# Attention's heads at later places in a hand-written order, and four small reorderings of copies, in a decoder block on one core

## The chip, the cores and the metric

The kernel runs on one core of a Trainium2 chip. The metric is the device time of one execution in microseconds (us); less is better. A core has a matrix engine (PE, with its weight loads as PEld), a vector engine (DVE), a scalar engine (ACT), GpSimd (POOL) and a queue that issues transfers (SP). Each engine works through its own list of instructions in order and waits where an instruction needs a result of another engine or of a transfer (DMA). Matmuls write to PSUM, which DVE and ACT read.

## What is computed

One layer for 512 tokens of width 2048, in float32: a token mixer, then a mixture of experts. The reference, cut to the mixer:

```python
h = _rms(x, attn_norm_g)
proj = h @ w_in        # q, six k/v of 4 groups, gates, 1024 pooled columns, 2 x 2048 merge columns
q = rope(rms(q)); k_slc = rope(rms(k_slc)); k_swa = rope(rms(k_swa))
kc, vc = compress(k_cmp), compress(v_cmp)          # 31 blocks
o = g0 * attn(q, kc, vc) + g1 * attn(q, k_slc, v_slc) + g2 * attn(q, k_swa, v_swa)
attn_branch = einsum("bshd,hde->bshe", o, w_head_out)      # 16 heads, 4 per k/v group
pooled = trailing means over 2, 4, 8, 16 positions, minus the token
pool_branch = einsum("bsgc,gce->bsge", pooled, w_pool) * pool_scale
merge = sigmoid(merge_logits)
y = merge[0] * attn_branch + merge[1] * pool_branch
x = x + y @ w_out
x = x + moe(rms(x))                                # 16 experts, two per token
```

With 512 tokens every block is selected and the window holds all keys, so both attentions are causal ones.

## The kernel before

Every float32 product is made of three matmuls: an operand is split into a rounded high part (ACT copies it, line 196) and the rest (DVE or POOL subtract, line 197), and `mm3` (lines 133 to 136) adds hi x hi, hi x lo and lo x hi. Tiles named `hi_...` and `lo_...` are those parts.

The order of the work is written by hand; no scheduler moves anything. `run(main, side)` walks a list of **main pieces**: one piece is one block of weights with its matmuls, in two parts of 12 matmuls of 512 columns (in some pieces one part of 24). After each part it takes one **step**: one entry from the list `deferred` (small DVE work of a piece that has just ended) and one entry from the list `side`. In the attention `side` holds the **slots** of `attention_slots`. A main piece may need a mark, and then `run` takes steps with no matmuls of a main piece between them until the mark is set.

The main pieces in this stretch are `qkv` (queries, keys and values of a group), `u` (pooled columns), `wp` (the pool's map, results `pm`), and `z0` to `z15` (merge columns of 128 output rows each). `z12` waits for the mark `att3`, `z8` for `att2`, `z4` for `att1`, `z0` for `att0`; head h of group g sets it in its last slot. When a `z` ends, DVE multiplies two tiles (line 947), ACT takes a tanh (948), DVE combines (949) and POOL or DVE adds (950).

A head counts its slots from its start w. `at_qk` writes the scores of query tile qt at w + 0, 2, 4, 6 into the one tile `S`; DVE adds the mask, takes the maximum and scales it (lines 772 to 776), ACT takes two exps (778), and only then may the next scores be written. `at_scale` makes the factors and scales the exps (`p`) one or two slots later (783 to 787). `at_T` transposes `p` at w + 9 to w + 14 into the one tile `tr`, which ACT (`pth`, 139) and DVE (`ptl`, 140) read; `at_pv` adds into the one tile `o` at w + 11 to w + 16, the last one copying `o` into `oh` and `ol`; `at_out` at w + 18 maps them (`a`), copies the result and stores it, and sets the mark after the fourth head. A group's start adds, from six slots ahead, transposes of queries (`at_q`, result `qT`) and keys (`at_k`) and the compressed branch (`at_c0` to `at_c4`). The table `PLAN` gives each group's start (`w0`) and the distances of its heads (`hp`).

`pool_out` reads each `pm` out of PSUM, on ACT (922) and DVE (920) in turn, into two buffers of the tag `ao`, which are shared with `a` and free again when the transfer out of them, issued by ACT (924, 831), has landed.

Of the kernel before, what the change touches and what calls it, by code (L numbers as in the profile page):

```python
# [22 lines left out]
NT = 4  # L23
# [3 lines left out]
NKV = 4  # L27
# [14 lines left out]
    'side': 'mnab.Bcd.gD.........h.k.iw',  # L42
    'main': 'ghqqKqKqKVqKVqVVq',
    'kvt': [1, 0, 1, 0],
    'w0': [7, 46, 85, 126],
    'hp': [[8, 8, 9], [8, 8, 9], [8, 8, 9], [8, 8, 8]],
    'q': -6,
    'pv': [11, 13, 14, 15, 16, 16],
    'T': [9, 10, 11, 12, 13, 14],
# [27 lines left out]
def hybrid_block_kernel(  # L77
# [10 lines left out]
    V, A, T, G = nc.vector, nc.scalar, nc.tensor, nc.gpsimd  # L88
# [7 lines left out]
    mix = mix_pool.__enter__()  # L96
# [7 lines left out]
    pools = {}  # L104
# [13 lines left out]
    def f(ap):  # L118
        return ap.bitcast(F32)
# [79 lines left out]
    deferred = []  # L199
# [82 lines left out]
    invb = mix.tile([128, S], F32, name="invb")  # L282
    rtmp = mix.tile([128, 24], F32, name="rtmp")
    gates = mix.tile([128, NT, 48], F32, name="gates")
    vcr = mix.tile([128, NKV, 64], F32, name="vcr")
    kcT = mix.tile([128, 128], F32, name="kcT")
    xt = [early.tile([128, D], F32, tag=f"x{t}", name=f"xt{t}") for t in range(NT)]
    sqx = early.tile([128, NT, 4], F32, name="sqx")
# [29 lines left out]
    hmask = mix.tile([128, 4], F32, name="hmask")  # L318
    icnt = mix.tile([128, 16], F32, name="icnt")
    sc = mix.tile([128, 5, 2, 8], F32, name="sincos")  # L320
    gain = mix.tile([128, 6, 64], F32, name="gain")
    posi = early.tile([128, 5], I32, name="posi")
    gainc = early.tile([128, 64], F32, name="gainc")
    w2k = early.tile([128, 2, 64], F32, name="w2k")
# [14 lines left out]

    def late_loads():  # L340
        q = nc.sync
        for i in range(4):
            q.dma_start(gain[:, i], q_norm_g.to_broadcast([128, 64]))
        q.dma_start(gain[:, 4], k_norm_slc_g.to_broadcast([128, 64]))
        q.dma_start(gain[:, 5], k_norm_swa_g.to_broadcast([128, 64]))
# [244 lines left out]
    def qkv(g):  # L590
        def loads(raw, k0):
            r = [(raw[:, :, 0:256], wcols(k0, 2, C_Q + 256 * g, 256))]
            for i, c in enumerate((C_KS, C_KW, C_VS, C_VW)):
                r.append((raw[:, :, 256 + 64 * i:320 + 64 * i], wcols(k0, 2, c + 64 * g, 64)))
            return r

        def done(ps):
            if g == 0:
                open_att()
            att = pools["att"]  # L600
            qn = QN[g] = att.tile([128, NT, 6, 64], F32, tag="qn", name=f"qn{g}")
            vt = VT[g] = att.tile([128, NT, 2, 128], F32R, tag="vt", name=f"vt{g}", bufs=2)
            ss = att.tile([128, 2, NT, 6], F32, tag="ss", name=f"ss{g}")
            for t in range(NT):
                pv = ps[t][:, 384:512].rearrange("p (b d) -> p b d", b=2)
                A.mul(qn[:, t].rearrange("p h d -> p (h d)"), ps[t][:, 0:384], inv[:, t:t + 1])
                A.mul(vt[:, t, :, 0:64], pv, inv[:, t:t + 1])
                V.scalar_tensor_tensor(vt[:, t, :, 64:128], pv, inv[:, t:t + 1], f(vt[:, t, :, 0:64]),
                                       op0=OP.mult, op1=OP.subtract)
            q2 = qn.rearrange("p t h d -> p (t h) d")  # L610
            q3 = qn.rearrange("p t h d -> p t (h d)")
            rs = ss[:, 1].rearrange("p t h -> p (t h)")
            s2 = ss[:, 0].rearrange("p t h -> p (t h)")

            def squares(u):
                sq = att.tile([128, 12, 64], F32, tag="th", name=f"sq{g}_{u}", bufs=3)
                us = slice(12 * u, 12 * u + 12)
                V.tensor_mul(sq, q2[:, us], q2[:, us])
                V.tensor_reduce(s2[:, us], sq, axis=AX.X, op=OP.add)

            def inverse():
                V.tensor_scalar(s2, s2, 1.0 / HD, EPS, op0=OP.mult, op1=OP.add)
                rsqrt(rs, s2, rtmp)

            def norm():
                V.tensor_tensor(q2, q2, rs[:, :, None].to_broadcast([128, NT * 6, 64]), op=OP.mult)

            def gains():
                V.tensor_tensor(q3, q3, gain.rearrange("p h d -> p (h d)")[:, None, :].to_broadcast([128, NT, 384]),
                                op=OP.mult)  # L630

            def rope():
                rt = att.tile([128, 4, NT, 6, 8], F32, tag="th", name=f"rt{g}", bufs=3)
                x1, x2 = qn[:, :, :, 0:8], qn[:, :, :, 8:16]
                co = sc[:, 0:4, 0, None, :].to_broadcast([128, NT, 6, 8])
                si = sc[:, 0:4, 1, None, :].to_broadcast([128, NT, 6, 8])
                V.tensor_mul(rt[:, 0], x1, co)
# [100 lines left out]
    def at_c4(g):  # L738
        att = pools["att"]
        smt = pools["sm"].rearrange("p t h n -> p t (h n)")  # L740
        ptc = tr_tile(f"pc{g}")
        for t in range(NT):
            T.transpose(ptc[:, t * 128:(t + 1) * 128], smt[:, t], ident)
        pch = att.tile([128, S], F32R, tag="pch", name=f"pch{g}")
        pcl = att.tile([128, S], F32R, tag="pcl", name=f"pcl{g}")
        evac_split(pch, pcl, ptc)
        PC[g] = (pch, pcl)
        vcf = att.tile([128, 4, 64], F32, tag="sm", name=f"vcf{g}")
        vcg = att.tile([128, 4, 128], F32R, tag="vcg", name=f"vcg{g}")
        V.tensor_tensor(vcf, vcr[:, g, None, :].to_broadcast([128, 4, 64]),  # L750
                        hmask[:, :, None].to_broadcast([128, 4, 64]), op=OP.mult)
        A.copy(vcg[:, :, 0:64], vcf)
        V.tensor_sub(vcg[:, :, 64:128], vcf, f(vcg[:, :, 0:64]))
        pools["vcg", g] = vcg

    def at_qk(head, qt):
        att, g = pools["att"], head // 4
# [42 lines left out]
    def at_pv(head, i):  # L800
        g, b = head // 4, i // 3
        pth, ptl, vt = pools["pth"], pools["ptl"], VT[g]
        if i == 0:
            o = pools["o"] = o_tile(f"o{head}")
            vcg, (pch, pcl) = pools["vcg", g], PC[g]
            T.matmul(o, vcg[:, head % 4], pch, start=True, stop=False)
            T.matmul(o, vcg[:, head % 4], pcl, start=False, stop=False)
        o = pools["o"]
        for j, o0, s0 in (((0, 0, 0),), ((1, 128, 768), (3, 256, 512)), ((2, 256, 1152),))[i % 3]:
            w = 512 - o0  # L810
            for pp in (pth, ptl):
                T.matmul(o[:, o0:512], vt[:, j, b, :], pp[:, s0:s0 + w], start=False,
                         stop=(i == 5 and pp is ptl))
        if i == 5:
            att = pools["att"]
            oh = att.tile([128, S], F32R, tag="oh", name=f"oh{head}")
            ol = att.tile([128, S], F32R, tag="ol", name=f"ol{head}")
            A.copy(oh, o)
            V.tensor_tensor(ol[64:128], o[0:64], f(oh[0:64]), op=OP.subtract)
            A.copy(ol[0:64], o[0:64])  # L820
            pools["oh"], pools["ol"] = oh, ol

    def at_out(head):
# [48 lines left out]
    def pool_in(g):  # L872
        w = 2 << g

        def done(ps):
            att = pools["att"]
# [18 lines left out]
                V.scalar_tensor_tensor(s, s, 1.0 / w, u, op0=OP.mult, op1=OP.subtract)  # L895
                V.tensor_tensor(s[:, :, 0:w - 1], e[:, :, 0:w - 1], u[:, :, 0:w - 1], op=OP.subtract)

            def halves():
                A.copy(ph, cur[0])
                V.tensor_sub(pl, cur[0], f(ph))  # L900
                PP[g] = (ph, pl)
                marks.add(f"pool{g}")

            deferred.extend([lambda st=1 << i: double(st) for i in range(g + 1)] + [mean, halves])

        return feature_major(f"u{g}", lambda raw, k0: [(raw, wcols(k0, 4, C_POOL + 256 * g, 256))], done)

# [689 lines left out]
```

## Time and profile before

| | |
|---|---|
| median of 3 runs (lowest, highest) | 1443.61 us (1442.37, 1444.62) |
| the profiled execution | 1442.58 us, span of its instructions 1440.8 us |
| PE busy | 1388.4 us, 96% of the span |
| DVE, ACT, POOL busy | 57%, 53%, 31% |
| mean granted PE clock | 0.984 of full speed |

The profiled execution is 1.03 us under the median. Attention's slots lie between some 170 and 812 us; the experts follow from 1100 us.

### The profile page before, as it was taken

To read this page: it belongs to the slowest core of one execution; us is meant where nothing else is said; L and a number is where in the kernel's file an instruction comes from. 1 tells how busy PE (TensorE), PEld (TensorE's weight loads), DVE (VectorE), ACT (ScalarE), POOL (GpSimd) and SP (SyncE) were. 2 spreads that over 40 slices of the span, in tenths; PEclk is the share of its full clock that TensorE was granted. 3 is DMA by queue.
4 is the path that set the end of the run, shared out by engine and by line. 5 is a ranking of instruction groups with operands and counts; after the bars stand their busy time and mean duration, and the time that the engine had idled before them with its cause. 6 is when DMAs were issued, how large, how long until landed. Compare 5 with 4: busy or idle time off the path is not lost.

```text
span 1440.8 us, 18395 instructions
## 1 busy us (share of the span) xinstructions
PE 1388.4 (96%) x6638; PEld 1138.2 (79%) x6638; DVE 825.1 (57%) x1258; ACT 765.6 (53%) x1289; POOL 445.4 (31%) x289
## 2 busy tenths in 40 slices
PE   8998999989999999999999999999999999999995
PEld 7877788778778788788888888888887777777774
DVE  4663773666463453555543202453255899999995
ACT  4543356564666465655665322332242687777784
POOL 0044342322333343243434455211021322222221
PEclk9999999999999999999999999999999999999998
DMA  6344233233333333343434453785675899999994
GB/s 224 94 115 123 80 102 87 77 107 85 91 116 111 92 93 87 96 117 97 109 110 125 117 141 108 224 326 166 226 252 175 279 362 367 367 358 354 330 363 84
DMA packets 193188, 249.88 MB, mean 173 GB/s; under 512 B 50384, under 2 KB 137536, under 8 KB 191264
## 3 DMA queue, kind: packets, MB, share of 16 engines
q1 hardware_dynamic: 176640, 199.13, 43.6%
q0 software_dynamic: 11808, 41.09, 10.0%
q10 hardware_dynamic: 4640, 8.40, 1.6%
q8 instruction: 54, 0.88, 0.3%
q14 instruction: 46, 0.38, 0.1%
HBM read 225.49 MB, written 35.65 MB: 181 GB/s over the span
## 4 chain that ended last, share of the span: by engine, by line
PE 79%; DVE 10%; ACT 6%; issue 2%; DMA 1%; POOL 1%; ACTq 0%; SPq 0%; POOLq 0%; DVEq 0%
PE z L134 7%; PE z L136 7%; PE z L135 7%; PE gu L136 4%; PE gu L134 4%; PE gu L135 4%; PE wo L134 4%; PE wo L136 4%; PE wo L135 4%; PE qkv L135 2%; PE qkv L134 2%; PE qkv L136 2%; PE dn L134 2%; PE dn L135 2%; PE dn L136 2%; PE xT L1245 2%
## 5 line engine op out<-in xcount | busy, mean ns | idle before, releaser
L197 POOL TENSOR_TENSOR lo_z<-raw_z,hi_z 128x1024 fp32r<-128x1024 f32 x64 | 153.4, 2401 | 200.5 <-ACT hi_z L196 192.8
L134 PE MATMUL z<-hT,hi_z 128*128 128x512 f32 x512 | 204.1, 399 | 0.0
L136 PE MATMUL z<-hT,lo_z 128*128 128x512 f32 x512 | 200.7, 392 | 0.0
L135 PE MATMUL z<-hT,hi_z 128*128 128x512 f32 x512 | 200.2, 391 | 0.0
L140 DVE TENSOR_TENSOR ptl<-pt,pth 128x512 fp32r<-128x512 f32 (+1 forms) x96 | 57.8, 602 | 177.0 <-ACT pth L139 176.8
L197 DVE TENSOR_TENSOR lo_gu<-raw_gu,hi_gu 128x2048 fp32r<-128x2048 f32 x64 | 146.8, 2294 | 9.8 <-ACT hi_gu L196 4.2
L196 ACT CAST hi_gu<-raw_gu 128x2048 fp32r<-128x2048 f32 x64 | 122.3, 1911 | 18.7 <-PE gu L136 9.9
L778 ACT ACTIVATE p<-s,m 128x128 f32<-128x128 f32 (+3 forms) x128 | 66.4, 523 | 115.6 <-DVE m L776 112.4
L197 POOL TENSOR_TENSOR lo_qkv<-raw_qkv,hi_qkv 128x1024 fp32r<-128x1024 f32 x28 | 70.6, 2521 | 173.8 <-ACT hi_qkv L196 148.6
L136 PEld LDWEIGHTS z<-hT,lo_z 128*128 128x128 f32 x512 | 96.5, 189 | 21.2
L135 PEld LDWEIGHTS z<-hT,hi_z 128*128 128x128 f32 x512 | 96.7, 189 | 18.6
L134 PEld LDWEIGHTS z<-hT,hi_z 128*128 128x128 f32 x512 | 96.9, 189 | 18.3
L134 PE MATMUL gu<-hi_gu,xh 128*112 128x512 f32 x256 | 106.4, 416 | 0.1
L134 PE MATMUL qkv<-hi_qkv,hT 128*128 128x512 f32 x256 | 103.5, 404 | 0.1
L135 PE MATMUL qkv<-lo_qkv,hT 128*128 128x512 f32 x256 | 101.4, 396 | 0.3 <-POOL lo_qkv L197 0.3
L136 PE MATMUL gu<-hi_gu,xl 128*112 128x512 f32 x256 | 101.7, 397 | 0.0
L136 PE MATMUL qkv<-hi_qkv,hT 128*128 128x512 f32 x256 | 101.5, 396 | 0.0
L134 PE MATMUL wo<-hi_wo,y 128*128 128x512 f32 x256 | 101.1, 395 | 0.0
L135 PE MATMUL gu<-lo_gu,xh 128*112 128x512 f32 x256 | 100.4, 392 | 0.0
L136 PE MATMUL wo<-hi_wo,y 128*128 128x512 f32 x256 | 99.8, 390 | 0.0
L135 PE MATMUL wo<-lo_wo,y 128*128 128x512 f32 x256 | 99.7, 389 | 0.0
L1313 POOL DMA_INDIRECT out_dram<-y,idx x18 | 60.1, 3337 | 107.7 <-ACT hi_gu L196 88.6
(419 smaller groups left out, 3193.7 us busy)
## 6 DMA issues: line engine op xcount, KB each, us to landing
raw_z<-in_w_in_dram SPq DMA_DIRECT2D x128, 256.0 KB
raw_gu<-in_w_expert_gate_dram SPq DMA_DIRECT2D x59, 512.0 KB
raw_gu<-in_w_expert_up_dram SPq DMA_DIRECT2D x59, 512.0 KB
raw_dn<-in_w_expert_down_dram SPq DMA_DIRECT2D x28, 1024.0 KB
raw_wo<-in_w_out_dram SPq DMA_DIRECT2D x32, 512.0 KB
raw_qkv<-in_w_in_dram SPq DMA_DIRECT2D x32, 256.0 KB
raw_qkv<-in_w_in_dram SPq DMA_DIRECT2D x128, 64.0 KB
raw_u<-in_w_in_dram SPq DMA_DIRECT2D x16, 512.0 KB
```

The costliest lines, as they stand in the source:

```text
L134: T.matmul(ps, ah, bh, start=start, stop=False)
L135: T.matmul(ps, ah, bl, start=False, stop=False)
L136: T.matmul(ps, al, bh, start=False, stop=stop)
L140: V.tensor_tensor(lo, src, f(hi), op=OP.subtract)
L196: A.copy(self.hi[sl], self.raw[sl])
L197: self.eng.tensor_sub(self.lo[sl], self.raw[sl], f(self.hi[sl]))
L778: A.activation(p[:, b], v[:, b], AF.Exp, bias=m[:, b:b + 1], scale=0.125, accum_out=m[:, 2 + b:3 + b])
L1245: T.transpose(pt[:, j * RS:(j + 1) * RS], self.xr[:, k0 * 128 + j:(k0 + 4) * 128:4], ident[0:RS, 0:RS])
L1313: ins = G.indirect_dma_start(out=dst, out_offset=bass.IndirectOffsetOnAxis(ap=idx, axis=0), in_=src, in_offset=None, bounds_check=n - 1, o ...
```

## The change

The starts and distances in `PLAN` change: group 0's heads stand 10, 10 and 9 slots apart and not 8, 8 and 9; the later groups start at slots 57, 102 and 139 and not at 46, 85 and 126, with heads 8 apart; and `z7` (`z13` in the list) goes ahead of `z8` (`z20`). Beside it, the compressed values are split once (`vhl`) and masked by four ACT instructions per group in place of two DVE and one ACT; the gains are applied by two DVE instructions with half the loads; `ol`'s copy on ACT stands ahead of the difference on DVE; and the pool's last entry of `deferred` is two entries.

```diff
-    'w0': [7, 46, 85, 126],
-    'hp': [[8, 8, 9], [8, 8, 9], [8, 8, 9], [8, 8, 8]],
+    'w0': [7, 57, 102, 139],
+    'hp': [[10, 10, 9], [8, 8, 8], [8, 8, 8], [8, 8, 8]],
...
-        'q31', 'z10', 'z11', 'z12', 'z20', 'z13', 'z21', 'z22', 'z23', 'z30', 'z31', 'z32', 'z33'],
+        'q31', 'z10', 'z11', 'z12', 'z13', 'z20', 'z21', 'z22', 'z23', 'z30', 'z31', 'z32', 'z33'],
...
-        V.tensor_copy(vcr, po[:, 0:256].rearrange("p (g d) -> p g d", g=4))
+        pv = po[:, 0:256].rearrange("p (g d) -> p g d", g=4)
+        A.copy(vhl[:, :, 0:64], pv)
+        V.tensor_tensor(vhl[:, :, 64:128], pv, f(vhl[:, :, 0:64]), op=OP.subtract)
...
-                V.tensor_tensor(q3, q3, gain.rearrange("p h d -> p (h d)")[:, None, :].to_broadcast([128, NT, 384]),
+                V.tensor_tensor(qn[:, :, 0:4], qn[:, :, 0:4], gain[:, 0, None, None, :].to_broadcast([128, NT, 4, 64]),
+                                op=OP.mult)
+                V.tensor_tensor(qn[:, :, 4:6], qn[:, :, 4:6], gain[:, None, 1:3].to_broadcast([128, NT, 2, 64]),
                                 op=OP.mult)
...
-        V.tensor_tensor(vcf, vcr[:, g, None, :].to_broadcast([128, 4, 64]),
-                        hmask[:, :, None].to_broadcast([128, 4, 64]), op=OP.mult)
-        A.copy(vcg[:, :, 0:64], vcf)
-        V.tensor_sub(vcg[:, :, 64:128], vcf, f(vcg[:, :, 0:64]))
-        pools["vcg", g] = vcg
+        vcg = pools["vcg", g] = att.tile([128, 4, 128], F32R, tag="vcg", name=f"vcg{g}")
+        for h in range(4):
+            A.mul(vcg[:, h], f(vhl[:, g]), hmask[:, h:h + 1])
...
             A.copy(oh, o)
+            A.copy(ol[0:64], o[0:64])
             V.tensor_tensor(ol[64:128], o[0:64], f(oh[0:64]), op=OP.subtract)
-            A.copy(ol[0:64], o[0:64])
...
-            def halves():
+            def half():
                 A.copy(ph, cur[0])
+
+            def rest():
                 V.tensor_sub(pl, cur[0], f(ph))
                 PP[g] = (ph, pl)
                 marks.add(f"pool{g}")
...
-            deferred.extend([lambda st=1 << i: double(st) for i in range(g + 1)] + [mean, halves])
+            deferred.extend([lambda st=1 << i: double(st) for i in range(g + 1)] + [mean, half, rest])
```

What the table moves, at three places. The first is DVE at group 1's queries (`q1`, subtracted out of `qT1`). Before, the transposes of head 3 (`pt3`) stand right behind:

```order
L665 TENSOR_TENSOR q1_0_2716<-qT1_2707,q1_0_2716 64x512
L665 TENSOR_TENSOR q1_1_2718<-qT1_2707,q1_1_2718 64x512
L665 TENSOR_TENSOR q1_2_2720<-qT1_2707,q1_2_2720 64x512
L665 TENSOR_TENSOR q1_3_2722<-qT1_2707,q1_3_2722 64x512
L900 TENSOR_TENSOR pl2_2598<-s2_4_2666,ph2_2597 128x1024
L140 TENSOR_TENSOR ptl_1242<-pt3_0_2748,pth_1240 128x512
L140 TENSOR_TENSOR ptl_1242<-pt3_1_2773,pth_1240 128x512
L679 TENSOR_TENSOR k2_1_2781<-kT1_2782,k1_1_2780 64x512 x4
L700 TENSOR_TENSOR kw2_1247<-kcT_95,kw1_1244 128x32
```

Now, on the same engine at the same work:

```order
L140 TENSOR_TENSOR ptl_1240<-pt3_4_2957,pth_1238 128x512
L140 TENSOR_TENSOR ptl_1240<-pt3_5_2979,pth_1238 128x256
L899 TENSOR_TENSOR pl3_2786<-s3_8_2917,ph3_2785 128x1024
L666 TENSOR_TENSOR q1_0_3018<-qT1_3009,q1_0_3018 64x512
L666 TENSOR_TENSOR q1_1_3020<-qT1_3009,q1_1_3020 64x512
L666 TENSOR_TENSOR q1_2_3022<-qT1_3009,q1_2_3022 64x512
L666 TENSOR_TENSOR q1_3_3024<-qT1_3009,q1_3_3024 64x512
L817 TENSOR_TENSOR ol3_3049<-o3_2869,oh3_3048 64x512
L680 TENSOR_TENSOR k2_1_3076<-kT1_3077,k1_1_3075 64x512 x4
```

All six transposes of head 3 are ahead of the queries now; the same holds for head 7 and group 2's queries.

The second is PE at the end of attention (`pt15` and `o15` are head 15's transposes and sum, `a15` its map). Before, a part of `z10` or `z11` stands between any two of its slots:

```order
L135 MATMUL z10_1_6728<-hT6_88,hi_z10_12_6782 128x512
L136 MATMUL z10_1_6728<-hT6_88,lo_z10_12_6783 128x512
L812 MATMUL o15_6823<-pth_1240,vt3_5117 128x256
L812 MATMUL o15_6823<-ptl_1242,vt3_5117 128x256
L797 MATMUL pt15_5_6903<-ident_77,p15_2_6626 128x128
L797 MATMUL pt15_5_6903<-ident_77,p15_3_6692 128x128
L134 MATMUL z10_0_6727<-hT7_89,hi_z10_12_6782 128x512
L135 MATMUL z10_0_6727<-hT7_89,hi_z10_12_6782 128x512
```

Now the last matmul of `z11` is followed by slot 176 (four sums `o15`, four transposes `pt15_4`), then by two more sums and two transposes, and then by these rows, with which the merge goes on (`z12`):

```order
L794 MATMUL pt15_5_7060<-ident_77,p15_3_6870 128x128
L809 MATMUL o15_6992<-pth_1238,vt3_4866 128x512
L809 MATMUL o15_6992<-ptl_1240,vt3_4866 128x512
L809 MATMUL o15_6992<-pth_1238,vt3_4866 128x384
L809 MATMUL o15_6992<-ptl_1240,vt3_4866 128x384
L809 MATMUL o15_6992<-pth_1238,vt3_4866 128x256
L809 MATMUL o15_6992<-ptl_1240,vt3_4866 128x256
L809 MATMUL o15_6992<-pth_1238,vt3_4866 128x256
L809 MATMUL o15_6992<-ptl_1240,vt3_4866 128x256
L824 MATMUL a15_7078<-oh15_7073,woh3_6155 128x512
L825 MATMUL a15_7078<-ol15_7074,wol3_6156 128x512
L134 MATMUL z12_0_7091<-hT0_82,hi_z12_0_6951 128x512
```

The last four slots of head 15 stand in a row, with no matmul of a main piece between; in the same way the last three of group 2's slots (head 11's last sums and `a11`, head 12's scores `s12_2`) stand together ahead of `z8`.

The third is DVE behind the last piece of `qkv2` (`sq2` and `ss2` are its norm, `pm3` the pool's map, `s4` and `m4` head 4's scores and maxima). Before:

```order
L618 TENSOR_TENSOR sq2_0_3474<-qn2_3459 128x768
L619 TENSOR_REDUCE ss2_3461<-sq2_0_3474 128x12
L920 TENSOR_SCALAR pool3_1_3503<-pm3_1_3496,cols_128 128x512
L618 TENSOR_TENSOR sq2_1_3506<-qn2_3459 128x768
L619 TENSOR_REDUCE ss2_3461<-sq2_1_3506 128x12
L819 TENSOR_TENSOR ol4_3516<-o4_3317,oh4_3515 64x512
L783 RECIPROCAL m5_3_3423<-m5_3_3423 128x2
L772 TENSOR_TENSOR s6_0_3525<-s6_0_3525,causal_129 128x256
L775 TENSOR_REDUCE m6_0_3530<-s6_0_3525 128x2
L776 TENSOR_SCALAR m6_0_3530<-m6_0_3530 128x2
L920 TENSOR_SCALAR pool3_3_3552<-pm3_3_3545,cols_128 128x512
```

Now:

```order
L617 TENSOR_TENSOR sq2_0_3324<-qn2_3309 128x768
L618 TENSOR_REDUCE ss2_3311<-sq2_0_3324 128x12
L769 TENSOR_TENSOR s4_2_3330<-s4_2_3330,causal_129 128x2x128
L772 TENSOR_REDUCE m4_2_3337<-s4_2_3330 128x2
L773 TENSOR_SCALAR m4_2_3337<-m4_2_3337 128x2
L919 TENSOR_SCALAR pool3_1_3366<-pm3_1_3359,cols_128 128x512
L617 TENSOR_TENSOR sq2_1_3369<-qn2_3309 128x768
L618 TENSOR_REDUCE ss2_3311<-sq2_1_3369 128x12
L780 RECIPROCAL m4_2_3337<-m4_2_3337 128x2
L919 TENSOR_SCALAR pool3_3_3394<-pm3_3_3387,cols_128 128x512
L621 TENSOR_SCALAR ss2_3311<-ss2_3311 128x24
L126 TENSOR_SCALAR ss2_3311<-ss2_3311 128x24
```

The mask and maximum of head 4's third scores stand ahead of `pool3_1` now, and `pool3_3` and the rest of the norm follow directly, ahead of head 4's last maximum; before, head 5's and head 6's work stood at these places.

## Rows read from the trace of the kernel before

**Rows 1.** PE's waits over the whole span: total us, times, longest us

```profile
PE pt L797 <- DVE ptl L140: 10.0, 6, 4.0
...
PE pt L797 <- ACT p L787: 4.1, 3, 2.2
PE s L769 <- ACT p L778: 3.1, 2, 2.6
```

**Rows 2.** Busy time by stretch: width, then PE, PEld, DVE, ACT, POOL, clock, DMA

```profile
216.00:318.00 102.00, 98.78 (x484) 81.91 (x483) 56.23 (x110) 61.28 (x151) 32.73 (x14) 1.00 0.31 88
318.00:328.00 10.00, 6.04 (x25) 4.89 (x24) 5.37 (x7) 6.73 (x11) 2.74 (x1) 0.83 0.38 103
328.00:480.00 152.00, 146.10 (x707) 120.64 (x706) 80.25 (x159) 85.92 (x205) 50.45 (x25) 1.00 0.37 101
480.00:492.00 12.00, 8.66 (x31) 6.95 (x30) 5.99 (x9) 8.28 (x14) 3.27 (x3) 0.72 0.28 88
492.00:602.00 110.00, 108.40 (x526) 90.53 (x524) 48.59 (x96) 61.69 (x149) 40.33 (x21) 1.00 0.37 94
602.00:870.00 268.00, 267.43 (x1279) 223.65 (x1280) 104.71 (x194) 133.21 (x281) 112.45 (x59) 1.00 0.41 115
```

**Rows 3.** Busy time in the two stretches of low clock, columns as in rows 2

```profile
324.00:327.50 3.50, 3.07 (x12) 2.79 (x13) 1.07 (x2) 1.64 (x3) 1.86 (x1) 0.51 0.11 18
484.40:491.30 6.90, 5.57 (x17) 4.75 (x18) 3.10 (x5) 4.33 (x8) 1.10 (x1) 0.51 0.39 115
```

**Rows 4.** DVE in order of time at group 1's queries: start, us, idle before

```profile
319.60 2.80 DVE L665 TENSOR_TENSOR q<-qT,q 64x512 fp32r<-64x512 f32 x4 [4.03 <-ACT q L662]
322.43 1.23 DVE L900 TENSOR_TENSOR pl<-s,ph 128x1024 fp32r<-128x1024 f32 x1
323.68 0.69 DVE L140 TENSOR_TENSOR ptl<-pt,pth 128x512 fp32r<-128x512 f32 x1
```

**Rows 5.** Groups of equal instructions between 600 and 870 us: count, busy us, mean ns

```profile
L196 ACT CAST hi_z<-raw_z 128x1024 fp32r<-128x1024 f32 x40 | 41.7, 1042 | 29.6 <-PE z L135 24.6 <-POOL th L950 5.1
...
L140 DVE TENSOR_TENSOR ptl<-pt,pth 128x512 fp32r<-128x512 f32 x24 | 16.6, 691 | 51.1 <-ACT pth L139 51.1
...
L772 DVE TENSOR_TENSOR s<-s,causal 128x256 f32<-128x256 f32 x20 | 8.4, 422 | 5.3 <-PE s L770 5.3
...
L778 ACT ACTIVATE p<-s,m 128x512 f32<-128x512 f32 x10 | 6.8, 685 | 12.3 <-DVE m L776 12.3
...
L775 DVE TENSOR_REDUCE m<-s 128x2 f32<-128x1024 f32 x5 | 6.1, 1225 | 0.2
...
L819 DVE TENSOR_TENSOR ol<-o,oh 64x512 fp32r<-64x512 f32 x7 | 4.8, 684 | 5.7 <-ACT oh L818 5.6
...
L818 ACT CAST oh<-o 128x512 fp32r<-128x512 f32 x6 | 3.5, 585 | 3.2 <-PE o L812 3.2
```

**Rows 6.** PE in order of time at the end of z11

```profile
825.39 0.39 PE L136 MATMUL z<-hT,lo_z 128*128 128x512 f32 x1
825.62 0.39 PE L134 MATMUL z<-hT,hi_z 128*128 128x512 f32 x1
```

**Rows 7.** DVE in order of time at the end of z11

```profile
825.14 1.37 DVE L947 TENSOR_TENSOR th<-z,invb 128x512 f32<-128x512 f32 x2 [17.58 <-PE z L136]
827.69 1.23 DVE L949 SCALAR_TENSOR_TENSOR ld<-th,ld 128x1024 f32<-128x1024 f32 x1 [1.18 <-ACT th L948]
```

**Rows 8.** PE behind the last matmul of qkv2

```profile
403.89 0.39 PE L812 MATMUL o<-pth,vt 128*128 128x512 f32 x1
```

**Rows 9.** DVE in order of time behind qkv2: start, us

```profile
405.98 0.35 DVE L608 SCALAR_TENSOR_TENSOR vt<-qkv,inv,vt 128x128 fp32r<-128x128 f32 x1 [0.38 <-ACT vt L607]
...
407.23 0.95 DVE L619 TENSOR_REDUCE ss<-sq 128x12 f32<-128x768 f32 x1
...
413.74 0.17 DVE L622 TENSOR_SCALAR ss<-ss 128x24 f32<-128x24 f32 x1
...
416.13 0.18 DVE L131 SCALAR_TENSOR_TENSOR ss<-rtmp,ss 128x24 f32<-128x24 f32 x1
```

**Rows 10.** ACT's issue of two transfers out of the pool's buffers

```profile
345.61 0.81 ACTq L924 DMA_DIRECT2D pdram<-pool  x2
```

**Rows 11.** DVE behind the first of these transfers

```profile
348.44 0.75 DVE L920 TENSOR_SCALAR pool<-pm,cols 128x512 f32<-128x512 f32 x1 [0.15 <-DMA pdram<-pool]
```

More of the change, by code (lines that the diff above doesn't have):

```diff
@@ L284, in hybrid_block_kernel @@
     gates = mix.tile([128, NT, 48], F32, name="gates")
-    vcr = mix.tile([128, NKV, 64], F32, name="vcr")
+    vhl = mix.tile([128, NKV, 128], F32R, name="vhl")
     kcT = mix.tile([128, 128], F32, name="kcT")
@@ L320, in hybrid_block_kernel @@
     sc = mix.tile([128, 5, 2, 8], F32, name="sincos")
-    gain = mix.tile([128, 6, 64], F32, name="gain")
+    gain = mix.tile([128, 3, 64], F32, name="gain")
     posi = early.tile([128, 5], I32, name="posi")
@@ L341, in late_loads @@
         q = nc.sync
[L342 to L345, printed above, removed]
+        for i, g_ in enumerate((q_norm_g, k_norm_slc_g, k_norm_swa_g)):
+            q.dma_start(gain[:, i], g_.to_broadcast([128, 64]))
         q.dma_start(gainc, k_norm_cmp_g.to_broadcast([128, 64]))
@@ L610, in done @@
             q2 = qn.rearrange("p t h d -> p (t h) d")
-            q3 = qn.rearrange("p t h d -> p t (h d)")
             rs = ss[:, 1].rearrange("p t h -> p (t h)")
@@ L747, in at_c4 @@
         PC[g] = (pch, pcl)
-        vcf = att.tile([128, 4, 64], F32, tag="sm", name=f"vcf{g}")
-        vcg = att.tile([128, 4, 128], F32R, tag="vcg", name=f"vcg{g}")
-        V.tensor_tensor(vcf, vcr[:, g, None, :].to_broadcast([128, 4, 64]),
-                        hmask[:, :, None].to_broadcast([128, 4, 64]), op=OP.mult)
-        A.copy(vcg[:, :, 0:64], vcf)
-        V.tensor_sub(vcg[:, :, 64:128], vcf, f(vcg[:, :, 0:64]))
-        pools["vcg", g] = vcg
+        vcg = pools["vcg", g] = att.tile([128, 4, 128], F32R, tag="vcg", name=f"vcg{g}")
+        for h in range(4):
+            A.mul(vcg[:, h], f(vhl[:, g]), hmask[:, h:h + 1])
     def at_qk(head, qt):
```

## Prediction

> **What bounds the kernel now.** The profiled execution is the base of the sum: 1442.58 us, 1.03 us under the median of 1443.61, so 1.03 is added back at the end. The page says that PE is busy 96% of the span. A kernel bound by PE can win where PE waits or runs at a lower clock, and nowhere else. The chain of waits on PE names whom it waits for in attention: 10.0 us in six waits for `ptl`, the longest 4.0; 4.1 us for the scaled `p`; 3.1 us for the exps [rows 1]. The busy time by stretch says where [rows 2]: PE's idle time (width less busy time) is 3.2 us in 216 to 318, 4.0 in 318 to 328, 5.9 in 328 to 480, 3.3 in 480 to 492, 1.6 in 492 to 602 and 0.6 in 602 to 870. Two of the stretches also show a clock under 1.00. Inside them 3.07 and 5.57 us of PE's busy time ran at 0.51 [rows 3], so 0.49 of it is lost: 1.5 and 2.7 us. All that the change can win is therefore 18.0 (216 to 602) + 4.2 = 22.2 us, and the 268 us behind 602, nearly without a wait, can only lose.
>
> **What is removed.** In 318 to 328 DVE subtracts group 1's queries for 2.80 us, having waited 4.03 for ACT's copies, then the pool's `pl` for 1.23, and only then `ptl`, for which PE waits [rows 4]. The stretch 480 to 492 is the same at group 2. In the changed order no transpose of `p` stands behind these queries. I take both idle times and the low clock behind them as gone: 4.0 + 1.5 + 3.3 + 2.7 = **-11.5 us**. The queries themselves then feed only work that is due slots later, and PE has main pieces meanwhile.
>
> **What takes its place in groups 0 and 1.** Two blocks of 24 matmuls now stand between scores of other heads, and elsewhere a wait meets fewer matmuls. A matmul takes 0.23 us of PE's time [rows 6], a part of 12 some 2.77.
>
> *A: `wp1`, group 0.* It follows `s2_3` directly and reads out `pm1` ahead of `a1`. From the end of `s2_3`: DVE does `ol` 0.69, mask 0.42, maximum 1.23 [rows 5] and a scale of 0.17 (a like instruction in [rows 9]), some 2.4; two exps of 0.69 with their sums, 4.0; a cast of 1.04, 5.0; `pool1_0` of some 0.7, 5.7. PE wants that PSUM buffer at 2.8, so it waits 2.9. The later `a1` needs an `ao` buffer, and `pool1_2` holds it until its transfer has landed; the chain to `p2_3` then ends some 2.1 us after PE wants it. A is 5.0 in place of the 3.2 idle in that stretch: **+1.8**. From below it is 1.3 (the transfer lands early), from above 7.
>
> *B: `qkv2`, `wp3`, `z0`, group 1.* Let T be the start of what follows `qkv2`'s last matmul, 403.89 before [rows 8]. The last `vt` ends at T + 2.4, the two halves of the squares (0.95 each) at T + 4.3 [rows 9]. Then, in the changed order, DVE does `s4_2`'s mask, maximum and scale (T + 5.85); ACT does two exps (7.3), a cast (8.2) and `pool3_0` (9.0); ACT issues two transfers in 0.81 [rows 10], T + 9.8. A transfer like these frees its buffer 2.0 us after the issue has ended: 345.61 + 0.81 = 346.42, and DVE goes on at 348.44 [rows 10, 11]. So `pool3_3` starts at T + 11.8 and ends at 12.6; the rest of the norm takes 2.57 (413.74 to 416.31, [rows 9]), T + 15.1; `s4_3`'s mask, maximum and scale end at 16.9, its exps at 18.5. PE waits 1.1 for `s4_3`, 0.8 for a buffer of `pm3`, reaches `s5_0` at T + 14.55 and waits 4.0 there, and 0.7 at `pt4_0`: 6.6 against 5.9 idle in 328 to 480, **+0.7**. Its bounds are 0 (the transfer is early and the 24 matmuls of `z0` hide the exps) and 11 (no wait overlaps another).
>
> *`pt8_0`* waits for the scaled `p` of head 8, some 2.4 by the longest such wait [rows 1] against 1.6 in 492 to 602: **+0.8**.
>
> **What the merge loses.** Behind 602 us nearly each wait of ACT or DVE lies under a part of `z`. The crammed slots take that cover away.
>
> *C: ahead of `z8`.* Three slots stand together behind `z7`. From the last matmul of a `z`, taken from z11 (T = 825.62, [rows 6]), DVE's two products end at T + 0.9, ACT's tanh at 2.1, DVE's combination at 3.3 [rows 7]. `z7` is one whose sum DVE adds (0.69): 4.0. Only then does DVE get to `s12_1`: mask 0.42, maximum 0.69, scale with the hand-overs 0.45, 5.6; two exps, 6.75. PE has 2.1 us of matmuls in these slots, so it is idle 4.6; `a11` waits another 0.65 for `ol`. **+5.3.**
>
> *D: ahead of `z12`.* Five slots with the last of head 15. By the same times the combination ends at T + 3.3; `ptl` (0.69, [rows 5]) at 4.0, since DVE does it behind; `pt15_5` waits because `tr` is one tile; its copies end at 5.4; then the last sums, `oh` 0.59, `ol` 0.69 [rows 5], and `a15` starts at T + 7.25, `z12` at 7.7. The matmuls in it take 3.1: **+4.6.** Bounds for C and D together are 5 (the tail of a `z` overlaps) and 14.
>
> **Low clock.** After the long waits at 320 and 482 us PE's granted clock is 0.51, the lower of its two levels, for some 3.5 us and 6.9 us, and it costs 1.5 and 2.7 us [rows 3]. The wait of 2.6 for the exps [rows 1], in the stretch 328 to 480, is followed by no fall: that row shows 1.00 [rows 2]. Two of my waits are as long as the one of 4.0, C's and B's at `s5_0`: 2 x 2.1 = **+4.2**, with the mean of 1.5 and 2.7. D is shorter piece by piece, as matmuls lie between its waits. The Trainium skill ("TensorE: Matmul & The Clock Gate", Part 1 on the HAM clock gate) says that the throttled clock is the array's default and that only sustained activity releases it. By that, each long gap is a candidate for a fall, and the rows at 320 and 482 agree while the stretch 328 to 480 does not; charging all four of A to D by it would add another 4.2.
>
> **Small edits.** `vhl`, the masks on ACT, the gains and the entry `half`/`rest` remove or move a few instructions of 0.2 to 1.3 us on DVE or ACT, which are busy 57% and 53% of the span. What of them ended a wait lies in the idle times already counted. `ol` ahead on ACT lets its copy lie beside DVE's difference (0.69, [rows 5]): a gain of at most 0.6 for a head where PE waits for it. I take 0, bounds -2 and +1.
>
> **The sum.** -11.5 + 1.8 + 0.7 + 0.8 + 5.3 + 4.6 + 4.2 = +5.9. 1442.58 + 5.9 = 1448.5; with 1.03 for the median, **1449.5 us**.
>
> **The rivals.** *Faster: A and B vanish.* If `pool3_3` has its buffer by T + 7.8 and not at 11.8, the norm and `s4_3`'s exps end 4 us sooner, just when PE comes to `s5_0`, and that wait and its low clock are gone; a like gain at `a1` clears `wp1`. Then all 22.2 us in 216 to 602 are won but for 2.4 at `pt8_0`: -22.2 + 2.4 + 5.3 + 4.6 + 2.1 (one fall of the clock, at C) = -7.8, or 1435.8. For it: of the small waits before, most hang on the places of heads 1 to 6, which all move. Against it: the transfers' 2 us [rows 10, 11] and DVE's chain behind `qkv2` [rows 9] are work that no table shortens.
>
> *No change: A and B cost what their stretches cost now*, and the clock falls once: -11.5 + 0.8 + 5.3 + 4.6 + 2.1 = +1.3, or 1444.9.
>
> *Slower still: each of A to D is followed by a low stretch*, four and not two: +10.1, or 1453.7, and up to 1457 with A and B at their upper bounds. The clock page of the Trainium skill speaks for this one; what speaks against it here is the 1.00 through the wait of 2.6 us.
>
> **How the numbers follow.** 0.2%, about what a measurement of this kernel tells from no change, is 2.9 us: faster is under 1440.7, slower over 1446.5. Chances: the forecast (1446 to 1452) 0.38, slower still 0.12, no change 0.22, faster 0.28. Of the forecast a little falls under 1446.5. So faster 0.28, same 0.24, slower 0.48. The likeliest case's own range is 1446 to 1452; the one that should hold the time 8 times in 10 reaches from the middle of the faster rival, 1436, to 1457, where only the ends of A and B are left out.
>
> **What would show it.** The removal is right if PE has no wait for `ptl` behind the queries of groups 1 and 2 and the clock there is 1.00. A is right if PE waits in `wp1` for `pool1_0` and at `pt2`; B if it waits some 4 us at `s5_0`; C and D if PE is idle some 5 us ahead of `z8` and again ahead of `z12`, so that the idle time behind group 2's start grows from under 1 to some 10 us. The prediction is wrong if the two crammed places cost under 2 us each, if the stretch from `s2_3` to `s5_0` has less idle time than the 9.1 us of before, or if a wait that I haven't named replaces the ones at the queries.

## The result, and the profile after

The changed kernel takes 1460.0 us (median of 3 runs, 1458.14 to 1462.24) against 1443.61: ratio 1.0115, 95% interval 1.0089 to 1.0141. It is 16.4 us slower, where 5.9 us were forecast, and lies above the range's end of 1457. Its profiled execution took 1460.0 us, its span 1458.3.

PE works through the same instructions up to some 213 us, and from the first matmul of the output projection on (912.66 us before, 929.52 now) the two kernels run alike to within some 1 us. So 16.9 us arise between these two points. The busy time by stretch, for each kernel from 216 us to the output projection (columns as in [rows 2]); first the kernel before:

```profile
216.00:912.60 696.60, 678.01 (x3234) 563.83 (x3233) 312.98 (x582) 369.42 (x819) 259.96 (x131) 0.99 0.38 106
```

And the changed kernel, the whole and then its parts:

```profile
216.00:929.50 713.50, 684.78 (x3234) 565.67 (x3233) 314.63 (x581) 370.09 (x827) 259.18 (x130) 0.98 0.37 103
...
216.00:318.00 102.00, 97.05 (x463) 80.08 (x462) 52.17 (x106) 54.48 (x134) 31.14 (x13) 0.98 0.31 86
318.00:328.00 10.00, 10.00 (x48) 8.34 (x47) 6.15 (x8) 6.84 (x14) 2.40 (x1) 1.00 0.36 91
328.00:480.00 152.00, 143.85 (x678) 118.18 (x677) 80.87 (x146) 81.97 (x186) 54.78 (x27) 0.98 0.37 105
480.00:492.00 12.00, 12.00 (x59) 9.81 (x58) 5.10 (x12) 6.11 (x17) 4.17 (x2) 1.00 0.47 133
492.00:602.00 110.00, 107.83 (x516) 88.91 (x516) 50.18 (x101) 57.94 (x129) 43.40 (x22) 1.00 0.38 96
602.00:890.00 288.00, 274.56 (x1303) 227.65 (x1302) 109.52 (x203) 152.44 (x341) 105.91 (x57) 0.98 0.36 103
```

Width less busy is PE's idle time: 18.6 us before, 28.7 now, **+10.1**. The same 3234 matmuls also took 678.0 us before and 684.8 now, **+6.8**. That second part is not a wait, and the forecast had it at nothing net. The two stretches at the queries, 318 to 328 and 480 to 492, with 4.0 and 3.3 us idle and a low clock before [rows 2], have no idle time and a clock of 1.00 now. The stretch behind 602 us has 13.4 us idle where there was 0.6.

PE's waits in the changed kernel (total us, times, longest us):

```profile
PE s L761 <- ACT p L775: 6.8, 1, 6.8
PE s L766 <- ACT p L775: 6.2, 2, 6.0
...
PE pt L794 <- DVE ptl L140: 4.8, 7, 2.5
PE pm L134 <- ACT pool L921: 4.2, 2, 3.4
PE pt L794 <- ACT p L784: 3.1, 3, 1.9
...
PE a L824 <- DVE ol L817: 1.9, 1, 1.9
...
PE qT L659 <- ACT p L775: 1.6, 1, 1.6
```

The waits for `ptl` fell from 10.0 to 4.8 [rows 1]; in their place stand those that the forecast named: for the scores behind `z0` (6.8), for the scores ahead of `z8` (6.0), at `pm1` (3.4), and ahead of `z12` (2.5 for `ptl`, 1.9 for `ol`). One had no name there: group 3's query transposes wait 1.6 for an exp.

What the clock did around these four places, A, B, C and D of the forecast (columns as in [rows 2]):

```profile
285.00:292.00 7.00, 3.60 (x11) 2.53 (x10) 1.86 (x3) 2.97 (x6) 2.36 (x1) 0.76 0.44 148
403.00:416.50 13.50, 6.65 (x24) 5.07 (x23) 11.81 (x26) 4.11 (x10) 2.59 (x1) 0.75 0.28 89
705.00:716.00 11.00, 4.99 (x19) 3.75 (x18) 7.38 (x15) 7.03 (x21) 1.80 (x3) 0.69 0.32 95
834.00:845.50 11.50, 8.26 (x26) 6.71 (x27) 2.42 (x4) 3.06 (x5) 4.12 (x3) 0.70 0.12 46
```

All four have a mean clock of 0.69 to 0.76: each long wait was followed by matmuls at the lower level, 1.2 GHz, not only two of them. The low stretches themselves, one at A, B and C each and two at D:

```profile
288.70:292.10 3.40, 2.84 (x7) 2.26 (x8) 0.00 (x0) 0.51 (x1) 2.35 (x1) 0.50 0.41 154
408.20:415.00 6.80, 4.24 (x11) 3.46 (x12) 6.73 (x7) 2.41 (x6) 2.59 (x1) 0.50 0.00 0
708.50:715.40 6.90, 3.52 (x9) 2.65 (x10) 4.70 (x10) 4.61 (x15) 1.80 (x3) 0.51 0.22 76
834.80:838.20 3.40, 2.83 (x10) 2.55 (x10) 0.94 (x2) 0.37 (x1) 1.80 (x2) 0.50 0.20 77
841.60:845.10 3.50, 3.50 (x10) 2.73 (x9) 0.00 (x0) 1.06 (x2) 1.91 (x1) 0.51 0.20 75
```

In them PE is busy 16.9 us, of which the lower clock costs half, **8.4 us**; in the kernel before it cost 4.2 [rows 3]. So the clock makes 4.2 of the +6.8. The other 2.6 us are busy time at 1.00.

Why B is longer than forecast stands in ACT's and DVE's order there (start, us, idle before and its releaser). ACT:

```profile
398.19 0.81 ACTq L923 DMA_DIRECT2D pdram<-pool  x2
...
402.52 0.69 ACT L921 ACTIVATE pool<-pm,cols 128x512 f32<-128x512 f32 x1 [1.98 <-DMA pdram<-pool]
```

DVE:

```profile
404.14 0.75 DVE L919 TENSOR_SCALAR pool<-pm,cols 128x512 f32<-128x512 f32 x1 [6.25 <-DMA pdram<-pool]
...
407.28 0.43 DVE L769 TENSOR_TENSOR s<-s,causal 128x256 f32<-128x256 f32 x1
407.74 1.23 DVE L772 TENSOR_REDUCE m<-s 128x2 f32<-128x1024 f32 x1
```

The two stores were issued by 399.0. The first buffer was free at 402.5 and the second at 404.1: 3.5 and 5.1 us, where [rows 10, 11] showed 2.0. DVE stood idle 6.25 us for it, with the norm and head 4's last maximum queued behind. The DMA engines were full in these microseconds (the last column but one is their share, the last one GB/s), while SP issued loads of `z`'s weights, 256 KB each:

```profile
397.19 4.14 SPq L171 DMA_DIRECT2D raw_z<-in_w_in_dram  x4
...
398.00:400.00 2.00, 1.79 (x8) 1.52 (x9) 0.00 (x0) 1.11 (x5) 2.00 (x1) 1.00 1.00 293
...
402.00:404.00 2.00, 1.92 (x9) 1.26 (x7) 0.00 (x0) 0.69 (x1) 0.00 (x0) 1.00 1.07 340
```

In the kernel before, the 2.0 us behind [rows 10] moved 262 GB/s, as much as the two stores of 256 KB alone:

```profile
346.40:348.40 2.00, 2.00 (x11) 1.63 (x10) 1.36 (x4) 0.45 (x2) 1.12 (x1) 1.00 0.70 262
```

And C, DVE ahead of `z8`:

```profile
703.29 0.87 DVE L735 TENSOR_TENSOR cst<-cst,gates 128x16 f32<-128x16 f32 x1
...
704.40 0.69 DVE L737 TENSOR_TENSOR sm<-sm,cst 128x512 f32<-128x512 f32 x1
...
705.09 1.27 DVE L946 TENSOR_TENSOR th<-z,invb 128x512 f32<-128x512 f32 x2
707.53 1.22 DVE L948 SCALAR_TENSOR_TENSOR ld<-th,ld 128x1024 f32<-128x1024 f32 x1 [1.18 <-issue]
708.79 0.69 DVE L949 TENSOR_TENSOR th<-ld 128x512 f32<-128x512 f32 x1
709.40 0.42 DVE L769 TENSOR_TENSOR s<-s,causal 128x256 f32<-128x256 f32 x1
```

The chain is the one of the forecast (products, tanh, combination, sum, mask), but it begins late: DVE still has the compressed branch's work of these slots (`cst`, `sm`) in front, so that the products start at 705.09, some 1.6 us behind the end of `z7`.

### The profile page after: what moved, and what is told of

The parts are those of the page before. It is cut to its first block, busy times and chain, and to the rows that moved or that the text cites. A ratio compares the mean times of both kernels' runs of the same rounds, so it can differ in the third digit from the quotient of the medians.

```text
span 1458.3 us, 18397 instructions
## 1 busy us (share of the span) xinstructions
PE 1395.4 (96%) x6638; PEld 1139.7 (78%) x6638; DVE 823.5 (56%) x1254; ACT 768.6 (53%) x1302; POOL 444.2 (30%) x289
## 4 chain that ended last, share of the span: by engine, by line
PE 80%; DVE 7%; issue 4%; ACT 4%; DMA 2%; POOL 1%; SPq 0%; POOLq 0%; ACTq 0%; DVEq 0%
PE z L134 6%; PE z L136 6%; PE z L135 6%; PE gu L136 4%; PE gu L134 4%; PE gu L135 4%; PE wo L134 4%; PE wo L136 4%; PE wo L135 4%; PE qkv L134 3%; PE qkv L135 3%; PE qkv L136 3%; PE o L809 2%; PE dn L134 2%; PE xT L1244 2%
```

## The experiments

Each ratio is to runs of the kernel before on the same chip, with its 95% interval. A difference to the changed kernel, which was timed on another occasion, is one of medians; by the ratios it comes out within some 1 us of that. Theory one of most expectations is that the places of the slots make the waits; its main rival at first was that the rewritten copies do.

**1. The table alone.** The kernel before with this edit only:

```diff
-    'w0': [7, 46, 85, 126],
-    'hp': [[8, 8, 9], [8, 8, 9], [8, 8, 9], [8, 8, 8]],
+    'w0': [7, 57, 102, 139],
+    'hp': [[10, 10, 9], [8, 8, 8], [8, 8, 8], [8, 8, 8]],
...
-        'q31', 'z10', 'z11', 'z12', 'z20', 'z13', 'z21',
+        'q31', 'z10', 'z11', 'z12', 'z13', 'z20', 'z21',
```

> The kernel before with the table alone changed (starts, distances, z7 ahead of z8); all copies as before. Theory one, the places of the slots make the waits: 1456 to 1461 us, PE waits of 5 to 7 us at the first scores behind z0 and ahead of z8, about 4.8 us ahead of z12. Rival, the copies make them (ol behind ACT's copy, gains in two DVE instructions): at most 1449 us, and the waits ahead of z0's scores and at pm1 are shorter by 2 us or more.

Measured: 1457.64 us, ratio 1.0105 (1.0088 to 1.0122). Its PE waits:

```profile
PE s L769 <- ACT p L778: 7.7, 3, 6.0
PE s L764 <- ACT p L778: 5.6, 1, 5.6
```

The same waits at the same places; ahead of `z12` PE waits 2.5 for `ptl` and 2.0 for `ol`. The table accounts for the slowdown.

**2. The copies alone.** The changed kernel with the three lines of the table set back.

> The changed kernel with the table of before; all copies, masks and gains as changed. Theory one: within 3 us of the kernel before (1440.5 to 1446.5), the waits for ptl of some 4 us at the queries of groups 1 and 2 are back, and none over 3 us stands elsewhere. Rival, the copies: over 1449 us.

Measured: 1440.88 us, ratio 0.9983 (0.9974 to 0.9993). The waits at the queries are back (9.0 us for `ptl` in five, the longest 3.4). The copies are a small gain of 1.0 to 3.8 us with this table, so the rival falls.

**3. No slots crammed.** The changed kernel with groups 2 and 3 earlier:

```diff
-    'w0': [7, 57, 102, 139],
+    'w0': [7, 57, 94, 131],
```

> The changed kernel with groups 2 and 3 eight slots earlier each (starts 7, 57, 94, 131), so that no slots stand together ahead of z8 and z12; groups 0 and 1 as changed. Theory one, the crammed slots are the larger half of the loss: PE's idle time behind group 2's start falls from 13.4 to under 4 us, the low clock there goes, and the time is 11 to 16 us less than the changed kernel's, less up to 6 us for group 2's queries, ahead of transposes again: 1446 to 1455. Rival, ACT and DVE are late in any case and the wait turns up at other slots: 1457 or more.

Measured: 1448.99 us, ratio 1.0046 (1.0030 to 1.0063), 11 us under the changed kernel. The waits at C and D are gone; B is still there:

```profile
PE s L761 <- ACT p L775: 6.1, 1, 6.1
...
PE qT L659 <- ACT p L775: 3.8, 2, 2.6
```

Two thirds of the loss hang on the starts of groups 2 and 3, as theory one said; the queries of group 2 cost 2.6 us and not 6. PE's idle time behind 602 us falls from 13.4 to 4.9, not under 4: the last heads have new waits of 0.6 to 0.8 us for `ptl`.

**4. The store behind B.** The changed kernel; the first two results of `wp3` are not stored, the others twice.

```diff
                 j = 4 * g + e
+                if g == 3:
+                    if e < 2:
+                        continue
+                    nc.scalar.dma_start(pdram[(j - 2) * 128:(j - 1) * 128, :], t)
                 nc.scalar.dma_start(pdram[j * 128:(j + 1) * 128, :], t)
```

> The changed kernel, but of wp3's four results the first two are not stored from their own buffers; the third and fourth are each stored twice, so the bytes stay the same and no buffer waits for a transfer (two blocks of pool values are those of others). Theory one, the wait of 7.0 us behind z0 hangs on a transfer that took 5.1 us: it falls to under 2 us, the clock behind it stays at 1.00, and the time is 6 to 9 us less than the changed kernel's, 1451 to 1454. Rival, DVE's norm and ACT's exps bound it anyway: the wait stays over 4 us and the time falls by at most 3 us.

Measured: 1453.54 us, ratio 1.0071 (1.0054 to 1.0087), 6.5 us under the changed kernel. The wait behind `z0` fell to 1.9, as DVE goes on at once:

```profile
397.86 0.73 DVE L919 TENSOR_SCALAR pool<-pm,cols 128x512 f32<-128x512 f32 x1
398.51 1.61 DVE L621 TENSOR_SCALAR ss<-ss 128x24 f32<-128x24 f32 x1
```

Theory one holds: waiting for the buffer's store made most of B's 6.8 us, and 1.9 stay without it.

**5. Matmuls in the waits.** The changed kernel with matmuls that nobody reads put into A to D, here at B:

```diff
+        if (head, qt) == (5, 0):
+            fill_mm(28)
```

> The changed kernel with matmuls of 512 columns, whose result nobody reads, put into the five long waits of PE: 14 at pm1, 28 behind z0, 24 ahead of the third scores of head 12, 10 and 8 in the last slots of head 15. They take somewhat less than the waits that they fill. Theory one, part of the loss is the low clock that follows a wait: the granted clock stays at 1.00 there and the time is 5 to 8 us less than the changed kernel's, 1452 to 1455. Rival, the low clock costs nothing, as other waits would take its place: within 1.5 us of the changed kernel.

Measured: 1455.37 us, ratio 1.0080 (1.0063 to 1.0097), 4.6 us under the changed kernel. The same four stretches:

```profile
285.00:292.00 7.00, 6.82 (x30) 5.21 (x30) 2.36 (x4) 3.10 (x7) 2.39 (x1) 1.00 0.48 149
403.00:416.50 13.50, 11.95 (x54) 9.36 (x52) 10.88 (x22) 3.63 (x9) 2.60 (x1) 1.00 0.31 99
705.00:716.00 11.00, 9.78 (x48) 7.76 (x47) 7.55 (x16) 6.42 (x19) 1.83 (x4) 1.00 0.33 97
834.00:845.50 11.50, 11.23 (x52) 8.80 (x51) 2.94 (x4) 3.48 (x6) 4.22 (x3) 1.00 0.13 47
```

The clock stays at 1.00 in all four, and the kernel is faster although PE does 84 matmuls more. So part of the loss is the low clock. The size of the gain is less sure: the two ratios' intervals overlap (1.0063 to 1.0097, 1.0089 to 1.0141). It is a little less than expected: two waits for the scaled `p` came up (at 296 and 415 us, 2.2 and 1.8 us) where the changed kernel has one of 0.4; there the slow matmuls had hidden them.

**6. All heads eight apart, no blocks of 24 between scores.** The changed kernel with `'w0': [7, 52, 94, 131]` and eights throughout `hp`.

> The changed kernel with all heads eight slots apart and starts 7, 52, 94, 131: group 1's queries come behind head 3's transposes, no slots are crammed, and neither wp1 nor wp3 nor z0 stands as a block of 24 between scores. Theory one, the gain forecast at the queries is real and A to D were the price: about 6 us for group 1's site and up to 6 for group 2's, 1430 to 1437. Rival, a wait at the queries is only moved to other slots: 1439 to 1445, as with the table of before.

Measured: 1439.79 us, ratio 0.9984 (0.9974 to 0.9993). The price of A to D is gone, but it is no faster than experiment 2: PE waits ten times for `ptl`, 9.6 us in all, the longest 2.3. Behind 700 us heads 12 to 14 have waits of 0.6 to 0.9 us, which neither the kernel before nor the changed one has there. The rival was right here: part of the gain at the queries went to other slots.

**7. Queries one slot behind the first transpose.** The changed kernel with `'w0': [7, 47, 87, 127]`, eights throughout.

> The changed kernel with all heads eight slots apart and starts 7, 47, 87, 127: a group's queries stand one slot behind the first transpose of the last head, as group 3's did in the kernel before, where PE was not idle. Theory one, the distance from the queries to the next transposes sets the wait: both waits of 3 to 4 us are under 1 us, and the time is 1430 to 1437. Rival, it is DVE's whole work in these slots: waits of some 4 us stay, 1439 to 1444.

Measured: 1446.08 us, ratio 1.0028 (1.0016 to 1.0041). Theory one was nearly right on the queries (0.9 and 1.3 us, where under 1 was expected) and wrong on the time, as the rival was:

```profile
PE pt L794 <- ACT p L784: 14.8, 6, 7.1
```

The 7.1 us stand at `pt5`, and DVE again waits for the pool's store there, 5.65 us: the wait of B at another head.

**8. Heads seven apart.** `'w0': [7, 49, 91, 133]`, sevens throughout.

> The changed kernel with heads seven slots apart and starts 7, 49, 91, 133: all queries come behind the last transposes and nothing is crammed. Theory one: the waits at the queries go, but heads closer by one slot make new ones at scores and scaled p, 1432 to 1445. Rival, spacing costs nothing: under 1432.

Measured: 1492.97 us, ratio 1.0348 (1.0330 to 1.0365). Both were wrong by far. A head's sum now starts in the slot in which `a` of the head before still has to be read out of the same tile:

```profile
PE o L803 <- ACT a L827: 23.0, 12, 3.9
```

**9. Another phase.** The changed copies with `'w0': [7, 46, 86, 126]`, eights throughout, `z8` ahead of `z7`.

> The changed kernel's copies with starts 7, 46, 86, 126 and all heads eight slots apart; z8 ahead of z7 as before. Queries of groups 2 and 3 come one slot behind the first transpose of the last head, those of group 1 in the same slot; heads keep the places against the blocks of z that group 3 had in the kernel before, where PE had no wait. Theory one, the place of the queries and that phase set the waits: at most 1.5 us at each query, no wait of 1 us in the later z's, 1432 to 1438. Rival, the store of the pool's buffer at wp3 holds DVE as in the run with starts 7, 47, 87, 127 (7.4 us at one place): 1441 to 1446.

Measured: 1434.26 us, ratio 0.9941 (0.9929 to 0.9954), faster than both kernels. The stretch from 216 us to the output projection, then the two with group 2's queries and the last heads:

```profile
216.00:906.10 690.10, 677.47 (x3239) 562.72 (x3238) 310.45 (x580) 370.39 (x828) 260.28 (x131) 1.00 0.39 107
...
480.00:500.00 20.00, 20.00 (x102) 16.76 (x101) 9.33 (x16) 7.72 (x14) 5.68 (x3) 1.00 0.40 106
700.00:800.00 100.00, 99.88 (x492) 83.68 (x492) 40.13 (x73) 56.33 (x126) 36.61 (x19) 1.00 0.38 106
```

PE's idle time is 12.6 us against 18.6 in the kernel before. All later starts lie one slot before those of experiment 7, and the time is 12 us less. The two runs also differ in `z8` ahead of `z7`, which was not tried by itself; the wait of 7.1 at the first transposes of head 5 is 1.9 here.

**10. Experiments 3 and 4 together.**

> The changed kernel with both the third and the fifth experiment's edits: no store of wp3's first two results from their own buffers (their pool values are those of others), and groups 2 and 3 eight slots earlier. Theory one, the two losses lie at different places and add: 11 us from the earlier starts and 6.5 from the store, 1441 to 1444. Rival, they share a wait: over 1446.

(The third and the fifth in this text are experiments 3 and 4 here.) Measured: 1446.62 us, ratio 1.0025 (1.0013 to 1.0037), 2.4 us under experiment 3 where 6.5 were expected. The rival's number was met, narrowly; its reason was not seen, as the waits at C and D are gone as in experiment 3. The wait at B is 1.9 as in experiment 4, but the clock fell behind it here and not there. Experiment 4's ten microseconds from that wait on:

```profile
403.00:413.00 10.00, 6.32 (x30) 4.76 (x29) 9.65 (x15) 5.25 (x14) 2.61 (x1) 1.00 0.51 160
```

The same matmuls in experiment 10:

```profile
404.80:414.80 10.00, 7.91 (x30) 5.94 (x29) 9.60 (x15) 5.29 (x14) 2.59 (x1) 0.83 0.51 160
```

Thirty matmuls took 6.3 us there and 7.9 here.

**11 and 12. A free buffer for the fourth result of `wp3`.** Experiments 9 and 6 with

```diff
-                t = att.tile([128, S], F32, tag="ao", name=f"pool{g}_{e}", bufs=2)
+                t = att.tile([128, S], F32, tag="sm" if (g, e) == (3, 3) else "ao", name=f"pool{g}_{e}",
+                             bufs=1 if (g, e) == (3, 3) else 2)
```

> The kernel with starts 7, 46, 86, 126, and the fourth result of wp3 in the buffer of the compressed scores, idle there, so that DVE has no store to wait for. Theory one, DVE stands behind the store: the wait at pt4 or pt5 behind wp3 falls by 2 to 7 us against the run without this edit and the time by 2 to 8 us, 1430 to 1436. Rival, ACT's third result still waits for a store and ACT's scales come as late: within 1.5 us of the run without it.

> The kernel with starts 7, 52, 94, 131 and the fourth result of wp3 in the idle buffer. Theory one: its wait of 2.5 us behind z0 shrinks to under 1, and the time is 1 to 3 us under 1439.8. Rival, no change within 1.5 us.

Measured: 1433.65 us, ratio 0.9939 (0.9926 to 0.9952), and 1439.05 us, ratio 0.9978 (0.9967 to 0.9988): 0.6 and 0.7 us under the runs without it, not clear of noise. At experiment 9's places the wait behind `wp3` stays at 1.9 us, for ACT's scales, as the rival said. At experiment 6's it falls from 2.3 to 1.5 us, not under 1, and the time by less than theory one said. At these places the store costs little.

## Why the prediction was wrong

The direction and all four places were right; the size was not: +5.9 forecast, +16.9 in the trace, 11.0 too little. 4.2 of that is idle time, 4.2 is clock, and 2.6 is busy time of PE at 1.00, for which the sum had no term. The steps that failed are the number of falls of the clock and, second, the store's 2.0 us at B.

- **The queries (-11.5)** were right. The stretches of [rows 3] are at 1.00 and without idle time, and experiment 2, with the old table, has the waits back.
- **A (+1.8)** was right, in part by luck: 4.95 us idle in 216 to 318 where 5.0 were forecast, but as 3.4 at `pm1` (2.9 forecast), 0.4 at `pt2` (2.1) and 1.1 at `pt1`, ahead of A, where the sum had nothing. `ol` ahead on ACT saved nothing: DVE's difference starts at 283.66, released by ACT's copy, which ended at 283.63. The two write one tile, and they still run one after the other.
- **B (+0.7)** was mis-sized: 8.2 us idle in 328 to 480 and not 6.6, with 6.8 and not 4.0 at `s5_0`. The step that failed is "a transfer like these frees its buffer 2.0 us after the issue has ended": here it took 5.1. Experiment 4 shows that the store holds the wait. Loads of `z`'s weights ran beside it (rows above), where nothing ran beside the stores of [rows 10]; that they make its length is only argued, as taking them away was not tried. A price from a stretch without other transfers doesn't hold in a full one. The Trainium skill ("DMA: Bandwidth & Descriptors", on the anatomy of one DMA) gives, for GpSimd's path, a fixed part of some 2.0 us and a part by size. By these figures of the Trainium skill 256 KB take some 2.6 us, an estimate; the 2.0 us of [rows 10, 11], on ACT's path, lie below that, and the 3.5 and 5.1 us at 399 above it.
- **`pt8_0` (+0.8)** was right: 2.2 us idle against 2.4.
- **C (+5.3)** was a little short: the scores wait 6.0 us and not 4.6 (and `a11` not at all, where 0.65 was forecast), since the crammed slots' own DVE work (`cst`, `sm`) stands ahead of the products, which I had begun at the end of `z7`.
- **D (+4.6)** was right: 2.5 and 1.9, with some tenths between.
- **Not in the sum**: group 3's queries, whose place against head 11 changed too, wait 1.6 us for exps. I had looked for the loss behind 602 us at C and D only.
- **Low clock (+4.2)** is the step that failed most. I charged two falls, because the wait of 2.6 in the kernel before "is followed by no fall", and none at D, because matmuls lie between its waits. The rows show falls at all four places, at D behind both waits, and they cost 8.4 us, the forecast's own 2.1 for each of four places (1.4, 2.1, 1.8 and 3.1). So the price was right on average, and the number of places was wrong. Experiment 5, which keeps PE busy, brings the clock back and, by medians, 4.6 us with it. The rival "slower still" had these 8.4 us, at 1453.7. The rule of the Trainium skill that the forecast cites ("TensorE: Matmul & The Clock Gate", Part 1) spoke for that rival, and the trace agrees; against it I had one row, a wait that the clock survived.
- **PE's time at 1.00** has no term in the sum and rose by 2.6 us. It goes with the table: between the first scores and the output projection PE's busy time, less what the low clock costs, is 704.1 us before, 706.9 now, 706.2 in experiment 1 (the table alone) and 703.8 in experiment 2 (the copies alone). What in the table makes it isn't known. It and the 4.2 of idle time at B, C and group 3's queries are the 6.8 us between that rival's +10.1 and the 16.9 measured.

The rivals that made the kernel faster or equal fell with A and B, which cost what the chain said or more. That the copies were the cause fell with experiments 1 and 2.

By their medians experiments 3 and 4 remove 11 and 6.5 us, and together 13.4. Between the first scores and the output projection the profiled executions say 10.4 and 4.6, and together 13.1. PE's idle time adds up there (7.4 and 3.7, together 11.2); of the 1.9 us that are missing 1.5 is clock, by the fall at B and others. The rest of the missing 4 us lies outside this stretch or in the spread between executions. What stays open are the 2.6 us of PE at 1.00, what makes the store at B so long, and what decides whether a wait of some 2 us brings a fall.

## What to carry to other kernels

In an order written by hand, slots that an engine must drain with no large work between them cost their whole chain over all engines: price them from the instructions queued ahead on each engine, the slots' own included. A long wait of PE costs more than itself, so charge the slow matmuls behind each of them, some 2 us for each place here; a single wait without a fall is no proof. Where two periodic streams meet (heads every eight slots, blocks of `z` every eight parts), their phase decides: one slot earlier, with the same spacing (and two blocks of `z` exchanged), was worth 12 us, and a few starts are better tried than derived.

## What was not expected of the hardware

- The same wait doesn't always bring a fall of the clock. Experiments 4 and 10 hold the same instructions up to group 2's start and wait 1.9 us at the same one; the clock is 1.00 behind it in one and 0.83 in the other (their rows above). In experiment 1 the clock stays at 1.00 behind D's waits of 2.5 and 2.0 us, and falls behind a wait of 1.95 at `pt8_0`. Experiments 9 and 11 both wait 2.1 us at the same transpose near 280 us. Experiment 9:

```profile
281.50:291.50 10.00, 7.89 (x32) 6.22 (x31) 5.38 (x15) 6.05 (x16) 2.38 (x2) 0.83 0.34 90
```

Experiment 11:

```profile
278.97:288.97 10.00, 7.90 (x38) 6.16 (x37) 6.04 (x17) 5.94 (x16) 2.39 (x1) 1.00 0.33 75
```

- A store of 256 KB took 2.0 us to free its buffer in one place and 5.1 in another of the same kernel family, with the DMA share at 0.70 in the first and near 1.0 in the second.
- A DVE instruction on 24 columns, 0.17 us in [rows 9], took 1.61 us in experiment 4 (its second row above). It ends at 400.12, and a subtraction of GpSimd (`lo_z`, from 397.70) at 400.09; whether the one waits for the other was not tried.
